# Branch products of a gated merge as fp16 products of Strassen's scheme, with all engines of the merge in written order

## The chip, the core and the metric

The kernel runs on one core of one Trainium2 chip. Its engines each have a queue of their own: TensorE (PE, matmuls; its weight loads are shown apart as PEld), VectorE (DVE), ScalarE (ACT), GpSimd (POOL), and SyncE (SP), which issues the DMAs. The metric is the device time of one execution in microseconds (us), as the median of the runs.

## The reference

One decoder layer for 512 positions and 16 meta tokens, width 1024, all in float32. Two attention branches (MLA and FoX, 16 heads of 64 each) are multiplied with gates and merged:

```python
y_mla = (o_mla * jax.nn.silu(z_mla)) @ w_br_mla[l]
...
y_fox = (o_fox * jax.nn.silu(z_fox)) @ w_br_fox[l]

mixed = (jax.nn.sigmoid(gate_a) * y_mla + jax.nn.sigmoid(gate_b) * y_fox) @ w_out[l]
h = h + rmsnorm(mixed, post_norm_g[l])
```

`gate_a` and `gate_b` are 1024 columns each of the projection `u @ w_in`. The change concerns the two products with `w_br_mla` and `w_br_fox`, each 512 x 1024 by 1024 x 1024, and the order of the work around them.

## The kernel before

Features lie on the partitions in tiles of 128, positions on the free axis. Float32 factors are cut into a high and a low part of type f32r (`wh`, `wl` for weights; `gh`, `gl` for activations), and a product is three matmuls per tile of 128 input features: high x high, high x low, low x high. A *unit* (`unit`) is one output tile of 128 features: 8 input tiles x 3 = 24 matmuls of 512 columns. Its weights come by a DMA of 512 KB into `wraw` (three buffers), ACT casts them to `wh` (L116), POOL subtracts to get `wl` (L92).

The stages in order: norm and small projections; attention, 16 stages of one head pair each (branch 1 is FoX, 0 is MLA), in which PE's order is written by hand and units of later work fill the time that the softmax takes; the merge; the output projection (`po`) with norm and store. In attention the weighted values are `ov` (fp16 matmuls, two heads in 64 columns each), and DVE writes `gT[br]` from them (L676), 128 x 8 x 512 f32 for each branch. The probabilities `pn` go through DMA transposes to `pt`, issued by SP.

There are 16 gate units (`pg`: tanh of half the gate goes to `th` on ACT, L409); four run in attention. The merge cuts `gT` into `gh`, `gl`, and then for each output tile i runs two branch units (`py`), multiplies on DVE (`tb`, L767), adds the branches (L770), cuts the sum into `mh` (ACT) and `ml` (DVE), and runs two of the gate units that are left. A scheduler sets the order of DVE, ACT, POOL and SP there; PE's order is that of the code.

Of the kernel before, what the change touches and what calls it, by code (L numbers as in the profile page):

```python
# [54 lines left out]
def block_kernel(ctx: ExitStack, tc: tile.TileContext, x, meta_tokens, pre_norm_g, w_in, fox_forget_b,  # L55
# [19 lines left out]
    uTh, uTl = (const.tile([128, KD, ROW + L - META], F32R, tag=n, name=n)[:, :, ROW - META :] for n in ("uTh", "uTl"))  # L75
    padp = ctx.enter_context(tc.tile_pool(name="padp", bufs=1, side="right"))
# [11 lines left out]
    def tps(*a):  # L88
        nc.tensor.transpose(*a)  # L89

# [60 lines left out]
    cqk = cctx.enter_context(tc.tile_pool(name="cqk", bufs=1, side="right"))  # L151
# [248 lines left out]
    gctx = ExitStack()  # L400
    gates = [(i, br) for i in range(KD) for br in range(2)]

    def gate_unit():

        i, br = gates.pop(0)

        def done(_, ps):
            ths[i, br] = thp.tile([128, S], F32, tag="th", name=f"th{i}{br}")
            nc.scalar.activation(ths[i, br], ps, AF.Tanh, scale=0.5)  # L409
        return unit(f"pg{i}{br}", win_w((O_GA, O_GB)[br], i), u_act, KD, REAL, done)  # L410


    with ExitStack() as att:
# [30 lines left out]
        gpool = gctx.enter_context(tc.tile_pool(name="gpool", bufs=1, side="right"))  # L444
        gT = [gpool.tile([128, KD, S], F32, tag=n, name=n) for n in ("gT0", "gT1")]
# [131 lines left out]
        def attention(br, pr):  # L577
# [88 lines left out]
            def values():  # L666
                po = ovp.tile([128, 512], F32, tag="ov", name=f"ov{nm_}")
                ph = [po[64 * h : 64 * h + 64] for h in range(2)]
                for h in range(2):
                    mm(ph[h], vms[br][0:80, h], pts[h][0:80, 0], start=True, stop=False)  # L670
                for j in range(4):
                    for i, (v, p) in enumerate(((0, 0), (0, 1), (1, 0))):
                        for h in range(2):
                            mm(ph[h][:, 128 * j :], vps[br][:, j, h, v], pts[h][:, 1 + 2 * j + p, 128 * j :], start=False,
                               stop=(j == 3 and i == 2))
                nc.vector.scalar_tensor_tensor(out=gT[br][:, pr, :], in0=po, scalar=vsc[br, pr], in1=sils[br, pr],  # L676
                                               op0=ALU.mult, op1=ALU.mult)

# [22 lines left out]
        for si, (br, pr) in enumerate(stages):  # L701
# [3 lines left out]
            if br == 1:  # L705

                za, zb = z_unit(1, pr), z_unit(0, pr)
                fill = za + vts[br, pr] + q + zb[:4] + k + zb[4:6] + v + zb[6:]
            elif not last:
                fill = q[:3] + vts[br, pr] + q[3:] + k + v  # L710
            else:
                g = gate_unit()
                fill = g[:4] + vts[br, pr] + g[4:] + gate_unit()
# [8 lines left out]
        ahead(first + sum(fills, []) + tail)  # L722
# [15 lines left out]
        run(tail[:4])  # L738
        va()
# [3 lines left out]
    fctx.close()  # L743
    rctx = ExitStack()
    with ExitStack() as mg:
        m1 = mg.enter_context(tc.tile_pool(name="m1", bufs=1))
        m2 = mg.enter_context(tc.tile_pool(name="m2", bufs=2))
        gh, gl = ([m1.tile([128, KD, S], F32R, tag=f"{n}{br}", name=f"{n}{br}") for br in (1, 0)][::-1]
                  for n in ("gh", "gl"))
        for br in (1, 0):  # L750
            for k in range(KD):
                nc.scalar.copy(gh[br][:, k], gT[br][:, k])
                split_lo(nc.vector, gl[br][:, k], gT[br][:, k], gh[br][:, k])
        gctx.close()
        cctx.close()
        mp = rctx.enter_context(tc.tile_pool(name="mp", bufs=1, side="right"))
        mh = mp.tile([128, KD, S], F32R, tag="mh", name="mh")
        ml = mp.tile([128, KD, S], F32R, tag="ml", name="ml")
        for i in range(KD):
            tb = {}  # L760
            for br in (1, 0):
# [3 lines left out]
                def done(_, py, br=br):  # L765
                    tb[br] = m2.tile([128, S], F32, tag=f"tb{br}", name=f"tb{i}{br}")
                    nc.vector.scalar_tensor_tensor(out=tb[br], in0=ths[i, br], scalar=1.0, in1=py, op0=ALU.add,  # L767
                                                   op1=ALU.mult)
                run(unit(f"py{i}{br}", get, lambda k, br=br: (gh[br][:, k, :], gl[br][:, k, :]), KD, [slice(0, S)], done))
            nc.vector.tensor_tensor(out=tb[0], in0=tb[0], in1=tb[1], op=ALU.add)  # L770
            nc.scalar.copy(mh[:, i], tb[0])
            split_lo(nc.vector, ml[:, i], tb[0], mh[:, i])
            for _ in range(2):
                if gates:
                    run(gate_unit())

        nc.scalar.activation(eps_t[0:1, 0:1], ths[KD - 1, 1][0:1, 0:1], AF.Square)
# [3 lines left out]
    with rctx, ExitStack() as og:  # L781
# [11 lines left out]

        def wout_unit(n, c, keep=None):
            return by_k(wunit([wout[:, 2 * c : 2 * c + 2, 512 * n : 512 * n + 512]], keep)[0], 2)
# [18 lines left out]
        for c in range(4):  # L814
            w = wout_unit(0, c)
# [68 lines left out]
```

## Time and profile before

| what | value |
|---|---|
| median of 3 runs | 632.11 us (631.9 to 633.5) |
| profiled execution, first to last instruction | 630.9 us |
| PE busy | 608.6 us (96%), granted clock 0.996 |
| PEld / DVE / ACT / POOL busy | 515.7 / 315.0 / 342.9 / 263.3 us |
| DMA queue | 84.67 MB, 53.0% of the engines' span |

The profiled execution's own time is known by its span alone; the runs lie 1.0 to 2.6 us above it, the median 1.2. The page gives busy time by engine, the chain that ended last (followed back from the last instruction through what released each step), groups of instructions with the mean length of one, and what ended the idle time before them. A matmul's length in the timeline includes its way through the array, so that neighbours overlap; the pace is read from start to start.

### The profile page before, as it was taken

Reading aid. Unit: us, or ns where it says so; the run is one execution under the profiler, and the core shown is the slowest. Engines: PE = TensorE matmul, PEld = TensorE weight load, DVE = VectorE, ACT = ScalarE, POOL = GpSimd, SP = SyncE. Lnnn points to the kernel's source line nnn. Section 1 sums busy time; section 2 is a strip of 40 time slices with the busy share of each in tenths; the row PEclk is TensorE's granted clock in tenths of the full one; section 3 lists DMA queues with packets and bytes.
Section 4 is the critical chain, followed back from the end, with each engine's and each line's share of the span. In section 5 each row is a group of like instructions: output and inputs, shape, how many; then the busy total and the mean of one; then the engine's idle time right before and its main releaser. Section 6 shows DMA issues by size and latency. Waiting matters only on the chain.

```text
span 630.9 us, 11084 instructions
## 1 busy us (share of the span) xinstructions
PE 608.6 (96%) x3890; PEld 515.7 (82%) x3890; DVE 315.0 (50%) x883; ACT 342.9 (54%) x774; POOL 263.3 (42%) x266
## 2 busy tenths in 40 slices
PE   3999989999999999999999999999999999999996
PEld 2879767988988889889889888878888888888885
DVE  3757557467476565674673765648222022113134
ACT  5656478378477575774784776757322232232321
POOL 3224633734344353343343443542544444444620
PEclk9999989999999999999999999999999999999999
DMA  8442657856656577467467665761532333333702
GB/s 284 123 84 54 138 147 188 205 143 153 168 135 137 145 148 163 113 162 174 101 157 175 116 153 149 158 166 38 162 93 80 97 99 100 101 100 113 255 34 100
DMA packets 204864, 85.38 MB, mean 135 GB/s; under 512 B 122684, under 2 KB 197820, under 8 KB 204808
## 3 DMA queue, kind: packets, MB, share of 16 engines
q1 hardware_dynamic: 204808, 84.67, 53.0%
q8 instruction: 30, 0.49, 0.3%
q14 instruction: 26, 0.21, 0.1%
HBM read 55.21 MB, written 4.26 MB: 94 GB/s over the span
## 4 chain that ended last, share of the span: by engine, by line
PE 89%; ACT 3%; DMA 3%; DVE 1%; issue 1%; POOL 1%; SPq 1%; DVEq 0%; POOLq 0%; ACTq 0%
PE py L86 14%; PE pg L86 14%; PE z L86 12%; PE v L86 8%; PE fk L86 7%; PE st L86 7%; PE po L86 7%; PE fq L86 7%; PE ov L86 5%; PE psm L86 3%; DMA pt<-pn 2%; PE mq L86 2%; PE mk L86 1%; PE vt L89 1%; DMA wsr<-in_w_in_dram 1%
## 5 line engine op out<-in xcount | busy, mean ns | idle before, releaser
L92 POOL TENSOR_TENSOR wl<-wraw,wh 128x1024 fp32r<-128x1024 f32 (+1 forms) x90 | 207.4, 2307 | 241.4 <-ACT wh L116 232.4
L116 ACT CAST wh<-wraw 128x1024 fp32r<-128x1024 f32 (+1 forms) x90 | 89.8, 1000 | 178.8 <-issue 84.1
L628 ACT ACTIVATE sf<-sf,nb 128x144 f32<-128x144 f32 (+3 forms) x128 | 71.9, 565 | 4.1 <-DVE nb L620 4.1
L655 ACT ACTIVATE pn<-sf,ri 128x128 f16<-128x128 f32 (+3 forms) x128 | 61.5, 551 | 15.0 <-ACT sf L628 14.8
L656 DVE SCALAR_TENSOR_TENSOR pn<-sf,ri,pn 128x128 f16<-128x128 f32 (+3 forms) x128 | 65.7, 553 | 7.9 <-ACT pn L655 7.9
L767 DVE SCALAR_TENSOR_TENSOR tb<-th,py 128x512 f32<-128x512 f32 x16 | 11.0, 686 | 107.4 <-PE py L86 107.4
L86 PE MATMUL z<-uTh,wh 128*128 128x512 f32 x128 | 51.4, 401 | 0.0
L86 PE MATMUL z<-uTh,wl 128*128 128x512 f32 x128 | 50.6, 395 | 0.0
L86 PE MATMUL z<-uTl,wh 128*128 128x512 f32 x128 | 50.4, 394 | 0.0
L86 PE MATMUL pg<-uTh,wh 128*128 128x512 f32 x128 | 50.1, 392 | 0.0
L86 PE MATMUL pg<-uTl,wh 128*128 128x512 f32 x128 | 49.8, 389 | 0.0
L86 PE MATMUL pg<-uTh,wl 128*128 128x512 f32 x128 | 49.8, 389 | 0.0
L86 PE MATMUL py<-gh,wh 128*128 128x512 f32 x128 | 49.8, 389 | 0.0
L86 PE MATMUL py<-gl,wh 128*128 128x512 f32 x128 | 49.8, 389 | 0.0
L86 PE MATMUL py<-gh,wl 128*128 128x512 f32 x128 | 49.8, 389 | 0.0
L620 DVE CUSTOM_DVE_ANT_0 sf<-st,maskt 128x272 f32<-128x272 f32 (+2 forms) x128 | 48.5, 435 | 0.0
L86 PE MATMUL st<-hlk,hlq 64*128 64x272 f32 (+3 forms) x480 | 48.0, 307 | 0.4 <-DVE nb L620 0.2
L642 POOL TENSOR_TENSOR mt<-sf,ri 128x96 f32<-128x96 f32 (+1 forms) x32 | 9.5, 297 | 83.7 <-DVE ri L637 62.1
L86 PEld LDWEIGHTS st<-hlk,hlq 64*128 64x128 f32 x480 | 35.4, 185 | 6.7 <-ACT wh L116 2.5
L86 PE MATMUL fk<-uTl,wh 128*128 128x256 f32 (+1 forms) x128 | 36.6, 286 | 0.0
L86 PE MATMUL fk<-uTh,wh 128*128 128x256 f32 (+1 forms) x128 | 36.5, 285 | 0.0
L86 PE MATMUL v<-uTh,wh 128*128 128x256 f32 (+1 forms) x128 | 36.5, 285 | 0.0
(186 smaller groups left out, 1449.4 us busy)
## 6 DMA issues: line engine op xcount, KB each, us to landing
wraw<-in_w_in_dram SPq DMA_DIRECT2D x56, 512.0 KB, 3.9
wraw<-in_w_br_fox_dram SPq DMA_DIRECT2D x8, 512.0 KB, 3.6
wraw<-in_w_br_mla_dram SPq DMA_DIRECT2D x8, 512.0 KB
wraw<-in_w_out_dram SPq DMA_DIRECT2D x8, 512.0 KB, 4.5
qpe_dram<-gT SPq DMA_DIRECT2D x8, 256.0 KB
QP<-qpe_dram SPq DMA_DIRECT2D x8, 256.0 KB, 2.8
pt<-pn SPq DMA_TRANSPOSE x128, 2.5
xr<-in_x_dram SPq DMA_DIRECT2D x4, 512.0 KB
```

What stands on the lines that cost most here:

```text
L86: nc.tensor.matmul(*a, **k)
L89: nc.tensor.transpose(*a)
L92: eng.tensor_tensor(out=lo, in0=src, in1=f32(hi), op=ALU.subtract)
L116: nc.scalar.copy(wh[:, :n], raw[:, :n])
L620: nc.vector.tensor_tensor_reduce(out=sf_of(h, b)[:, c0 : c0 + w], in0=ps[h][:, o : o + w], in1=maskt[:, m0 : m0 + w], scale=-scale, scalar ...
L628: nc.scalar.activation(sf, sf, AF.Exp, bias=sums["nb"][:, h, b : b + 1], scale=-1.0, accum_out=sums["su"][:, h, b : b + 1])
L642: nc.gpsimd.tensor_tensor(out=mt, in0=src, in1=ri.unsqueeze(3).broadcast_to([128, 2, nb_, META]), op=ALU.mult)
L655: nc.scalar.activation(hi, sf, AF.Copy, scale=rib)
L656: nc.vector.scalar_tensor_tensor(out=lo, in0=sf, scalar=rib, in1=hi, op0=ALU.mult, op1=ALU.subtract)
L767: nc.vector.scalar_tensor_tensor(out=tb[br], in0=ths[i, br], scalar=1.0, in1=py, op0=ALU.add, op1=ALU.mult)
```

## The change

The branch products `py` are made in another way. Two output tiles (a *pair*, 256 features) at a time, the 2 x 2 blocks of weights (halves of the input features by the two output tiles) and activations (halves of the features by halves of the positions) are combined by Strassen's scheme in Winograd's form: 7 products of blocks instead of 8. Each block or sum of blocks is scaled by a power of two and cut into two fp16 halves. A product is 4 input tiles x 3 matmuls of 256 columns. The scales come from the chip: ACT squares the data and sums along the rows (`sumsq`), a matmul with ones adds over the partitions (`total`, tiles `sum`), DVE keeps the exponent (`pow2_scale`, three or four small operations). Every sum of blocks is made in place, in `yraw` (raw weights, now 1 MB per DMA) by DVE, in `gT[1]` by POOL, in `gT[0]` by DVE. ACT makes the high half (`hi`), DVE the low half (`lo`). Results are added in three banks (`yx`, `yy`, `yz`; products 1, 6, 5, 3 add up in `yx`), with copies of partial results on ACT (`cp`, L940 to L944) and additions and gating on DVE (L821, L933). The two branches have different scales; `mixed` brings them together when `mh` and `ml` are cut.

In the merge the order of all five queues is now written out as a string of tokens: a digit is a product, `g` three matmuls of a gate unit, `G` the cast of a gate unit's weights, `ah1`/`al1` the high and low half of operand 1 for the next pair, `as` a sum, `aq` a square, `aS` a scale, `L` a load, `B1h1` the same for the activations of branch 1. The gate units are ordered by branch, FoX first; FoX's four pairs come first, then MLA's. One sum of blocks of `gT[1]` (POOL), its squares (ACT) and its scale are made in attention's last stages. The attention's own order is otherwise the same on each engine.

```diff
+    def sumsq(src, acc):
+
+        with nc.allow_low_precision(reason="a bound for a power of two"):
+            nc.scalar.activation(junk[:, : int(np.prod(src.shape[1:]))], src, AF.Square, accum_out=acc)
+
+    def total(cols):
+
+        ps = acc(f"sum{uid[0]}")[:, 0:1]
+        uid[0] += 1
+        for i, c in enumerate(cols):
+            mm(ps, ALL1, c, start=(i == 0), stop=(i == len(cols) - 1))
+        return ps
+
+    def pow2_scale(s, inv, sq):
+
+        nc.vector.tensor_scalar(out=inv.bitcast(I32), in0=sq.bitcast(I32), scalar1=0x7F000000, scalar2=1,
+                                op0=ALU.bitwise_and, op1=ALU.logical_shift_right)
+        nc.vector.tensor_scalar(out=inv, in0=inv, scalar1=2.0 ** 50, scalar2=2.0 ** -60, op0=ALU.mult, op1=ALU.max)
+        nc.vector.reciprocal(s, inv)
...
-    gates = [(i, br) for i in range(KD) for br in range(2)]
+    gates = [(i, br) for br in (1, 0) for i in range(KD)]
...
+                if br and pr % 2:
+                    g2 = gT[1][:, pr - 1 : pr + 1].rearrange("p k s -> p (k s)")
+                    sumsq(g2, gss[:, 1, pr // 2 : pr // 2 + 1])
...
+                def g_scale():
+                    pow2_scale(sg[1], isg[1], total([gss[:, 1, c : c + 1] for c in range(4)]))
+                    b1, b2 = (gT[1][:, 0:4, 256 * c : 256 * c + 256] for c in range(2))
+                    b22 = gT[1][:, 4:8, 256:512]
+                    nc.gpsimd.tensor_tensor(out=b2, in0=b22, in1=b2, op=ALU.subtract)
+                fill = g[:4] + vts[br, pr] + g[4:] + g2[:4] + [(100, g_scale)] + g2[4:]
...
-        for i in range(KD):
-            tb = {}
-            for br in (1, 0):
-                def get(br=br):
-                    return by_k(wunit([wbr[br][:, :, 128 * i : 128 * i + 128]])[0], KD)
...
-                run(unit(f"py{i}{br}", get, lambda k, br=br: (gh[br][:, k, :], gl[br][:, k, :]), KD, [slice(0, S)], done))
...
+        mg.enter_context(tc.manual_schedule(engines={E_.PE, E_.Activation, E_.DVE, E_.Pool, E_.SP}))
...
+            def hi(self, n):
+                t = self.pool.tile([128, 2, K2, self.width], F16, tag="op", name=f"{self.name}{n}")
+                nc.scalar.activation(t[:, 0], self.quads[n], AF.Copy, scale=self.s)
+                self.ops[n] = t
+
+            def lo(self, n):
+                t = self.ops[n]
+                nc.vector.scalar_tensor_tensor(out=t[:, 1], in0=self.quads[n], scalar=self.s, in1=t[:, 0], op0=ALU.mult,
+                                               op1=ALU.subtract)
...
+            def product(self, n):
+                ps = self.y if n in (7, 4) else self.z if n == 2 else self.x
+                a, b = W[self.br, self.p].ops[n], TB[self.br].ops[n]
+                first = n in (1, 7, 2)
+                q = 0
+                for k in range(K2):
+                    for i, j in ((0, 0), (0, 1), (1, 0)):
+                        mm(ps, a[:, i, k], b[:, j, k], start=(first and q == 0), stop=(q == 3 * K2 - 1),
+                           skip_group_check=not first)
+                        q += 1
...
+        std = ("1 {0} 7 2 aS 6 ah1 ah7 al1 g ah2 al7 g 4 as6 {2} al2 ah6 g as5 ah4 g 5 as3 al6 ah5 g bq0 al4 g ah3 3 bs7 "
+               "al5 g bq1 {1} al3 g cL")
...
+        go(2, std.format("J2", "J3 B0s7", "G"))
...
+        go(5, std.format("M00", "M01", "G"))
+        go(6, std.format("M10", "M11", ""))
+        go(7, "1 7 O 6 M20 2 O 5 M21 4 O 3 M30 M31")
```

How the order of three queues changes at the places that matter below. First PE, where a gate unit meets branch work; before, at the first branch unit:

```order
L86 MATMUL pg_5472<-uTh,wh_5468 128x512
L86 MATMUL pg_5472<-uTl,wh_5468 128x512
L86 MATMUL pg_5472<-uTh,wl_5469 128x512
L86 MATMUL py_5589<-gh_5540,wh_5585 128x512
L86 MATMUL py_5589<-gl_5542,wh_5585 128x512
L86 MATMUL py_5589<-gh_5540,wl_5586 128x512
```

PE now, in the first pair, at the end of product 6 (`aop` is an operand of weights, `bop` of activations, both fp16):

```order
L92 LDWEIGHTS aop_5678
L92 MATMUL yx_5705<-bop_5637,aop_5678 128x256
L92 MATMUL pg_5770<-uTh,wh_5627 128x512
L92 MATMUL pg_5770<-uTl,wh_5627 128x512
L92 MATMUL pg_5770<-uTh,wl_5628 128x512
```

f32r and fp16 now alternate within every pair; before, PE stayed with f32r. Next DVE, from the last `gT` to the first merged tile before:

```order
L676 SCALAR_TENSOR_TENSOR gT_678<-ov_5485,vsc_5223,sil_5244 128x512
L92 TENSOR_TENSOR gl_5542<-gT_679,gh_5540 128x512 x8
L92 TENSOR_TENSOR gl_5543<-gT_678,gh_5541 128x512 x8
L767 SCALAR_TENSOR_TENSOR tb_5614<-th_5422,py_5589 128x512
L767 SCALAR_TENSOR_TENSOR tb_5647<-th_791,py_5622 128x512
L770 TENSOR_TENSOR tb_5647<-tb_5647,tb_5614 128x512
L92 TENSOR_TENSOR ml<-tb_5647,mh 128x512
```

DVE now, at the end of the first pair (`cp_5708<-yx_5705` is the addition of product 5):

```order
L836 SCALAR_TENSOR_TENSOR bop_5768<-gT_687,gsc,bop_5768 128x1024
L836 SCALAR_TENSOR_TENSOR aop_5774<-yraw_5584,ysc_5586,aop_5774 128x512
L821 TENSOR_TENSOR yraw_5588<-yraw_5588 128x4x128
L821 TENSOR_TENSOR cp_5708<-yy_5706,cp_5708 128x256
L112 TENSOR_SCALAR ysc_5590<-sum_5816 128x1
L114 TENSOR_SCALAR ysc_5590<-ysc_5590 128x1
L115 RECIPROCAL ysc_5590<-ysc_5590 128x1
L880 TENSOR_SCALAR ysc_5590<-ysc_5590,gsc 128x1
L836 SCALAR_TENSOR_TENSOR aop_5823<-yraw_5588,ysc_5590,aop_5823 128x512
L821 TENSOR_TENSOR cp_5708<-yx_5705,cp_5708 128x256
L933 SCALAR_TENSOR_TENSOR th_5436<-th_5436,cp_5708 128x512
```

That addition, which frees the bank for product 3, stands behind the scale and the first low half of the second pair. Last ACT, before, from the end of attention on:

```order
L409 ACTIVATE th_5525<-pg_5472 128x512
L752 CAST gh_5540<-gT_679 128x512 x4
L752 CAST gh_5541<-gT_678 128x512 x8
L116 CAST wh_5654<-wraw_5652 128x1024
L116 CAST wh_5687<-wraw_5685 128x1024
L116 CAST wh_5720<-wraw_5718 128x1024
L771 CAST mh<-tb_5647 128x512
```

ACT now, for the operands of the second pair (`aop_5823` to `aop_5876`) up to the copies of that pair's first products:

```order
L831 ACTIVATE aop_5823<-yraw_5588,ysc_5590 128x512
L831 ACTIVATE aop_5825<-yraw_5588,ysc_5590 128x512
L831 ACTIVATE aop_5828<-yraw_5588,ysc_5590 128x512
L831 ACTIVATE aop_5846<-yraw_5588,ysc_5590 128x512
L831 ACTIVATE aop_5853<-yraw_5588,ysc_5590 128x512
L100 ACTIVATE junk,yss_5785<-yraw_5782 128x1024
L831 ACTIVATE aop_5858<-yraw_5588,ysc_5590 128x512
L831 ACTIVATE aop_5876<-yraw_5588,ysc_5590 128x512
L448 ACTIVATE th_5883<-pg_5770 128x512
L940 COPY cp_5893<-yx_5890 128x256
L942 COPY cp_5893<-yy_5891 128x256
```

The copy of product 1 of the second pair stands behind all seven high halves of that pair, a square and a tanh.

More of the change, by code (lines that the diff above doesn't have):

```diff
@@ L150, in block_kernel @@
     cctx = ExitStack()
[L151 removed]
+    cqk = cctx.enter_context(tc.tile_pool(name="cqk", bufs=1))
     cTh = cqk.tile([128, 3, L], F32R, tag="cTh", name="cTh")
@@ L720, in block_kernel @@
         tail = gate_unit()
-        ahead(first + sum(fills, []) + tail)
+        mgates = [Gate() for _ in gates[:]]
+        ahead(first + sum(fills, []) + tail + mgates[0].steps)
         run(first)
@@ L738, in block_kernel @@
         run(tail[:4])
+        mgates[0].make()
+        mgates[1].load()
         va()
@@ new lines, in block_kernel, with mixed @@
+        mix = {}
+        pre = []
+        def mixed(p, part):
+            w = W[0, p]
+            for i in (2 * p, 2 * p + 1):
+                m = ths[i, 1]
+                if part == 0:
+                    nc.vector.scalar_tensor_tensor(out=m, in0=m, scalar=w.r, in1=ths[i, 0], op0=ALU.mult, op1=ALU.add)
+                    nc.scalar.activation(mix["h"][:, i], m, AF.Copy, scale=w.inv)
+                else:
+                    nc.vector.scalar_tensor_tensor(out=mix["l"][:, i], in0=m, scalar=w.inv, in1=f32(mix["h"][:, i]),
+                                                   op0=ALU.mult, op1=ALU.subtract)
```

209 lines of the change are left out of this document (178 added, 31 removed).

## The prediction

> **What bounds the kernel now.** I read the chain that ended last first, then the busy time by stretch, then single instructions. The chain, in order of time (start, length, what; us):
>
> ```profile
> 424.32 1.97 PE ov L86 x26
> 426.29 2.95 PE pg L86 x12
> 429.24 10.88 PE py L86 x48
> ...
> 559.80 21.76 PE py L86 x96
> 581.56 43.92 PE po L86 x216
> ```
>
> Between the last attention matmul (`ov`) and the output projection (`po`) it is nothing but gate units (`pg`) and branch units (`py`). Busy time by engine in that stretch (PE, PEld, DVE, ACT, POOL, clock, DMA share, GB/s):
>
> ```profile
> 426.20:581.40 155.20, 155.20 (x688) 128.53 (x685) 41.84 (x46) 50.16 (x67) 69.74 (x28) 1.00 0.34 96
> ```
>
> PE is never idle there, DVE is busy for 27% and ACT for 32%, and the DMA engines for a third. So the merge lasts as long as its matmuls: `py` is six pieces of 10.88 and one of 21.76, 87.04 us for 384 matmuls of 512 columns (0.2267 us each), `pg` the other 68. A change of `py` counts in full for as long as the other engines keep up.
>
> **The products on PE.** 384 f32r matmuls of 512 columns become 8 pairs x 7 products x 12 = 672 fp16 matmuls of 256. Pace is start to start, since the lengths overlap. fp16 in `ov`, and f32r of 256 columns near the end, from the timeline (start, length, instruction):
>
> ```profile
> 425.63 0.49 PE L86 MATMUL ov<-pt,vp 128*64 128x256 f16 x6
> 425.74 0.44 PE L86 MATMUL ov<-pt,vp 128*64 128x256 f16 x6
> ...
> 425.96 0.33 PE L86 MATMUL ov<-pt,vp 128*64 128x128 f16 x5
> ...
> 622.84 0.28 PE L86 MATMUL po<-wh,mh 128*128 128x256 f32 x1
> ...
> 625.20 0.28 PE L86 MATMUL po<-wl,mh 128*128 128x256 f32 x1
> ```
>
> Three fp16 steps of 256 columns take 0.33 us, 0.110 each (two heads side by side in 64 columns). Twenty f32r steps take 2.36, 0.118 each. fp16 weights are half as wide, so I take 0.110: 672 x 0.110 = 73.9 us, **-13.1**; at 0.118 it would be 79.3, -7.7.
>
> Weight loads have their own row (the second figure is the mean in ns):
>
> ```profile
> L86 PEld LDWEIGHTS py<-gh,wh 128*128 128x128 f32 x128 | 24.0, 188 | 5.0
> L86 PEld LDWEIGHTS <-vp 128*64 128x64 f16 x384 | 21.2, 110 | 8.4
> ```
>
> For f32r a load of 188 ns stands in every 227 ns of a stream in which 512 columns alone take 217 (fp16, below): loads go on behind matmuls. The Trainium skill, "TensorE: Matmul & The Clock Gate", section "The mechanism" of Part 3, says that loads overlap matmuls in flight only when they go to another row group. Its section "Back-to-back issue gap" gives 81 ns for 128 columns and 131 for 512, from which 98 ns for 256 is an estimate of that page and 672 of them 66 us, a gain of 21. The trace agrees with neither: full-height loads hide, and the 512-column steps stand at 217 ns below. The rows decide.
>
> **Changes of number type.** After `ov` PE changes between f32r and fp16 56 times (28 each way). What a change costs, from rows:
>
> ```profile
> 412.72 0.60 PE L89 MATMUL vt<-ident,vT 128*128 128x128 f32 x4
> 413.15 0.27 PE L89 MATMUL vm<-ident,vT 128*128 128x128 f32 x1
> 413.50 0.40 PE L86 MATMUL pg<-uTl,wh 128*128 128x512 f32 x1
> ...
> 423.94 0.39 PE L86 MATMUL pg<-uTh,wl 128*128 128x512 f32 x1
> 424.25 0.41 PE L86 MATMUL ov<-pt,vm 80*64 80x512 f16 x2
> 424.49 0.39 PE L86 MATMUL ov<-pt,vp 128*64 128x512 f16 x2
> ...
> 426.22 0.50 PE L86 MATMUL pg<-uTh,wh 128*128 128x512 f32 x1
> 426.56 0.39 PE L86 MATMUL pg<-uTl,wh 128*128 128x512 f32 x1
> ```
>
> Plain f32 transposes come 0.108 apart (four in 0.43). From the last of them to the second `pg` matmul are 0.35 us, of which 0.108 and 0.227 are the two at their pace: 0.016 for the change. Into `ov` it is dearer: 0.31 and 0.24 instead of 0.227 and 0.217, 0.11 more; out of it 426.22 less 425.96 less three steps of 0.055, 0.10, and 0.34 instead of 0.227, 0.11: 0.31 for a round trip. But `ov` loads half the array's columns, the new products all of them, as the transposes do. So 0.03 each, nearest to the full-width row: **+1.7**; ends 56 x 0.016 = 0.9 and 28 x 0.31 = 8.7.
>
> **Sums for the scales.** 24 matmuls of one column with a weight load each. No row has such; nearest are the transposes at 0.108 (2.6) and 128 columns of fp16 at 0.055 (1.3). I take **+2.0**.
>
> **The cuts on ACT, DVE and POOL.** Their prices (line, engine, operation, tiles, count, then busy us and mean ns of one, idle before):
>
> ```profile
> L655 ACT ACTIVATE pn<-sf,ri 128x512 f16<-128x512 f32 x32 | 21.5, 715 | 7.3 <-ACT sf L628 7.1
> L322 ACT ACTIVATE hn<-ht 128x1024 f32<-128x1024 f32 x3 | 3.2, 1060 | 0.0
> L808 ACT ACTIVATION_READ_ACCUMULATOR jk<-po 128x1 f32 x9 | 1.7, 194 | 0.0
> L116 ACT CAST wh<-wraw 128x1024 fp32r<-128x1024 f32 x80 | 83.6, 1048 | 159.7 <-issue 82.6 <-PE py L86 33.9 <-PE pg L86 17.6
> L409 ACT ACTIVATE th<-pg 128x512 f32<-128x512 f32 x16 | 9.4, 589 | 0.0
> L228 ACT CAST hlk<-fk 128x256 fp32r<-128x256 f32 x8 | 2.9, 364 | 0.0
> L656 DVE SCALAR_TENSOR_TENSOR pn<-sf,ri,pn 128x512 f16<-128x512 f32 x32 | 22.7, 748 | 7.9 <-ACT pn L655 7.9
> L325 DVE SCALAR_TENSOR_TENSOR hn<-ht,st,gb 128x1024 f32<-128x1024 f32 x3 | 3.8, 1279 | 0.0
> L92 DVE TENSOR_TENSOR gl<-gT,gh 128x512 fp32r<-128x512 f32 x16 | 9.8, 685 | 0.9 <-ACT gh L752 0.8
> L92 DVE TENSOR_TENSOR ml<-tb,mh 128x512 fp32r<-128x512 f32 x8 | 16.9, 2112 | 5.5 <-ACT mh L771 5.5
> L810 DVE TENSOR_TENSOR yo<-po,gp 128x256 f32<-128x256 f32 x2 | 0.8, 425 | 2.7 <-ACT jk L808 2.7
> L534 DVE TENSOR_SCALAR vsc<-vsc 128x1 f32<-128x1 f32 x16 | 2.5, 154 | 0.6
> L92 POOL TENSOR_TENSOR wl<-wraw,wh 128x1024 fp32r<-128x1024 f32 x80 | 194.3, 2432 | 217.9 <-ACT wh L116 212.6 <-DMA pt<-pn 3.5 <-PE po L86 1.8
> ...
> 437.26 8.01 POOL L92 TENSOR_TENSOR wl<-wraw,wh 128x1024 fp32r<-128x1024 f32 x3 [12.29 <-ACT wh L116]
> 440.88 2.14 DVE L770 TENSOR_TENSOR tb<-tb,tb 128x512 f32<-128x512 f32 x1
> ```
>
> Note the two TENSOR_TENSOR rows of DVE: the same 512 elements take 0.69 us when POOL is idle and 2.1 while POOL has one of its own, as the last two rows show side by side.
>
> An ordinary pair then costs: PE 84 x 0.110 + a gate unit 5.44 + 0.4 = 15.1. ACT 7 high halves x 0.715, 2 squares x 1.25, 3 copies x 0.364, tanh 0.589, `wh` 1.048: 10.2. DVE 7 low halves x 0.748, 4 sums x 0.685, the scale 4 x 0.154, 5 operations on 256 columns x 0.425, one of 512 x 0.748: 11.5. Both fit behind PE, which is why I cost them at nothing there. Cover is thin at two places.
>
> *The start (pairs 0 and 1).* Count from the last `ov` matmul (t = 0). The halves of gT1 write into memory that attention still holds, so they begin behind its last DVE instruction:
>
> ```profile
> 426.40 0.75 DVE L676 SCALAR_TENSOR_TENSOR gT<-ov,vsc,sil 128x512 f32<-128x512 f32 x1 [8.02 <-PE ov L86]
> ```
>
> at 0.9. ACT has three halves of 1024, a tanh and two squares: 3.2 + 0.6 + 2.5, at 7.2. PE comes to the first sum at 2.7 + 21 x 0.227 = 7.5: no wait. It has 27 gate matmuls until 13.9, and the first cut is ready at about 11.8: no wait. In pair 0 product 3 waits for DVE's addition of product 5 (both use one bank), and in DVE's queue that stands behind the first low half of pair 1. From 11.1 on, DVE has 8 low halves (6.0), 3 of 1024 (3.8), 4 sums (2.7, and 1.4 more for one beside POOL's `gT` sums), 3 x 0.425, a scale (0.6): 15.8, and ACT's high half after the scale 0.7; so 27.6, with the addition 28.0. PE is there at 13.9 + 6 x 1.32 + 21 x 0.227 + 0.5 = 27.1: wait 0.9. In pair 1 product 6 waits for the copy of product 1, which on ACT stands behind 7 more halves, a square and a tanh: from 27.1, 5.0 + 1.25 + 0.6 + 0.4 = 34.3 and 1 for DVE's sums between; PE arrives at 28.0 + 1.32 + 0.7 + 3.96 = 34.0: wait 1.3. The next addition, behind a sum beside `wl`: 1.0. Semaphores and the rest of pairs 1 to 3: 0.8. Together **+4.0**. Ends 1 and 8 (three more sums at 2.1).
>
> *Pairs 5 and 6.* Merging adds 4 x 0.748 to DVE and 0.3 to the scale: 14.8 of 15.1, and 16.2 with one sum beside `wl`. **+1.5**; ends 0 and 4.
>
> **Joints.** The first `po` matmul now waits for the gating of the last product (0.18 from PE to DVE as in the row above, 0.43, semaphores): **+0.7**. Before, nothing stood there. The transposes ahead of the last `ov`:
>
> ```profile
> L661 SPq DMA_TRANSPOSE pt<-pn x128: 1178/1247/2295, 86.6 to 421.0; - x128
> DMA to landing us min/median/max: 2.3/2.5/4.5
> ```
>
> The last is issued at 421.0 and lands 2.5 later, 0.7 before PE needs it. On SP a 1 MB load now stands among them: one more issue, at most the 1.2 of a transpose, and its bytes ahead of theirs. PE itself comes 0.3 later, by its four sums. **+0.3**; ends 0 and 3 (the longest landing instead of the median, and an issue). Four squares of 1.25 in attention delay ACT's `pn`; in the first three of those stages five units stand between scores and `ov` where the last has three, and in the last SP's 1.2 per transpose is what sets the landing: nothing.
>
> Sum: -13.1 + 1.7 + 2.0 + 4.0 + 1.5 + 0.7 + 0.3 = **-2.9**. The profiled execution's span of 630.9 becomes 628.0; the median of the runs lies 1.2 above that span, so 632.1 becomes **629.2 us**.
>
> **Rivals.**
> - *The cuts hide wholly.* The DVE and ACT terms (5.5) fall away if DVE's sums seldom meet POOL, which in an ordinary pair has only 2.4 of 15.1 us. For it, a row of the same operation (least, median and greatest ns):
>
> ```profile
> L770 DVE TENSOR_TENSOR tb<-tb,tb x8: 691/692/2139, 440.9 to 582.3; 128x512 f32<-128x512 f32 x8
> ```
>
> Most of these met no POOL. Against: `ml` met it each time. 629.2 - 5.5 = 623.7 us. Chance 0.22.
> - *A change of type costs what it costs around `ov`* (ends on the other side): 8.7 instead of 1.7, so 636.2. It decides from (2.9 + 1.7) / 28 = 0.16 us a round trip. For it: the three rows of `ov`, the only fp16 there is. Against: the transposes. Chance 0.14.
> - *DVE becomes the bound:* two of four sums meet POOL in each pair, 11.5 + 2 x 1.4 = 14.3 and in merging pairs 17.6 against PE's 15.1. Pairs 5 and 6 then cost 5.0 instead of 1.5, and one more dear sum in the first pairs 1.4: 634.1. For it: `ml`. Against: POOL's 2.4 in 15.1. Chance 0.17.
> - *Loads do not hide behind fp16 matmuls of 256 columns.* At the 110 ns of the `vp` row each product matmul would take 0.22: 74 more, 703. The f32r streams speak against it. Chance 0.02. The rule of the Trainium skill on row groups, cited above, would have it so.
> - *No change:* the products run at 0.118, 5.4 dearer, and the start's waits of 4.0 lie behind that: -1.5. Chance 0.03.
>
> **The numbers.** My forecast has 0.42; its own range is 625 to 633. 0.3% is 1.9 us, about what a measurement tells from none. Faster: 0.22 and 0.27 of mine, 0.49. Same: 0.11 of mine, 0.05 of the third rival, 0.03: 0.19. Slower: 0.04, 0.14, 0.12, 0.02: 0.32. The range: 621.5 (cuts hidden, changes at 0.016, sums at 1.3) to 638 (`ov`'s price and a little more waiting).
>
> **What would show it.** The products' steps at 0.110 in the timeline, and PE's busy time in the merge near 145; idle PE before `po` of 0.7; idle PE of 1 to 2 us in each of the first two pairs, ended by DVE's `cp` addition and ACT's `cp` copy; `yraw` sums on DVE with a mean between 0.7 and 1.1. It is wrong if steps after a gate start 0.1 or more late, if `yraw` sums take 2 us throughout, or if PE waits in pairs 2 to 4.

## The result, and the profile after

The changed kernel took 651.7 us (median of four runs, 648.7 to 653.0) where the kernel before took 632.5. The medians lie 19.2 us apart; the ratio over the single executions, which the table below uses too, is 1.0286 (95% interval 1.0254 to 1.0319), or 18.1 us more. The forecast was 2.9 less, and the range ended at 638. The profiled execution took 650.5, with a span of 648.7.

The chain of work that ended last, after the change, at the places that were shown of before (start, length, what; us):

```profile
431.90 2.02 PE ov L92 x22
...
476.40 0.60 DVE yraw L821
477.00 2.79 DVE aop L836
479.80 0.60 DVE yraw L821
480.40 0.35 DVE cp L821
480.78 1.47 PE yx L92 x12
482.26 1.40 PE pg L92 x6
483.66 1.32 PE yx L92 x12
484.98 1.31 PE yy L92 x12
...
505.49 0.13 PE sum L92 x6
...
596.49 46.73 PE po L92 x216
```

Where the chain of before was nothing but matmuls, VectorE (DVE) now stands in it. Cut at the end of `ov` and the start of `po`, the span has three stretches: the last `ov` ends 7.6 us later (433.92 for 426.29; forecast 0.3), the merge is 7.3 longer (162.57 for 155.27; forecast 3.2 shorter), `po` 2.8 longer (46.73 for 43.92; forecast no change). These sum to 17.7 of the spans' 17.8.

Busy time in the merge (columns as in the prediction), then PE's waits there, in all, times, longest:

```profile
433.90:596.50 162.60, 146.76 (x994) 118.39 (x993) 143.59 (x210) 103.12 (x166) 45.78 (x17) 1.00 0.30 90
```
```profile
PE yx L92 <- DVE cp L821: 7.6, 6, 2.9
PE po L92 <- DVE th L933: 4.5, 1, 4.5
PE yx L92 <- ACT cp L940: 2.2, 3, 1.7
...
PE yy L92 <- DVE aop L836: 1.3, 1, 1.3
```

PE has 146.76 us of work, near the forecast (145), and stands idle for 15.8 more. For 13.6 of these it waits for DVE: six times for the addition that frees a product's bank, once for the gating ahead of `po`, and for operands; the other 2.2 are ACT's copies. What makes DVE late shows where two engines are read side by side, in the second pair, while the third pair's operands are cut (timeline):

```profile
475.33 0.74 DVE L836 SCALAR_TENSOR_TENSOR aop<-yraw,ysc,aop 128x512 f16<-128x512 f32 x1
...
476.87 2.38 POOL L118 TENSOR_TENSOR wl<-wraw,wh 128x1024 fp32r<-128x1024 f32 x1 [12.94 <-ACT wh L142]
476.92 2.87 DVE L836 SCALAR_TENSOR_TENSOR aop<-yraw,ysc,aop 128x512 f16<-128x512 f32 x1
...
480.32 0.41 DVE L821 TENSOR_TENSOR cp<-yx,cp 128x256 f32<-128x256 f32 x1
...
480.78 1.47 PE L92 MATMUL yx<-bop,aop 128*128 128x256 f16 x12 [0.98 <-DVE cp L821]
```

A low half of this size takes 0.74 us alone and 2.87 beside one of POOL's weight subtractions. POOL's ends at 479.25, the low half at 479.79, 0.54 later, as if it had stood still until POOL was done. Behind it in DVE's queue is the addition into `cp`, and behind that PE. Over all such low halves (line, engine, operation, count: least, median, greatest ns):

```profile
L836 DVE SCALAR_TENSOR_TENSOR aop<-yraw,ysc,aop x56: 737/744/2881, 445.8 to 584.0; 128x512 f16<-128x512 f32 x56
```

They are busy for 55.5 us, 13.8 more than 56 at the median. The Trainium skill has this ("SBUF — State Buffer", section "Who interferes with whom"): a DVE instruction with two inputs in SBUF and a GpSimd one that reads SBUF exclude each other, and the first holds the way for its whole length. The rows agree; an addition into `cp`, one of whose inputs lies in PSUM, keeps its 0.42 beside POOL in the next rows (at 589.47).

At the end of the merge (timeline):

```profile
589.40 5.11 POOL L118 TENSOR_TENSOR wl<-wraw,wh 128x1024 fp32r<-128x1024 f32 x2 [0.17 <-PE yx L92]
589.47 0.42 DVE L821 TENSOR_TENSOR cp<-yx,cp 128x256 f32<-128x256 f32 x1
589.81 5.24 DVE L969 SCALAR_TENSOR_TENSOR ml<-th,ysc,mh 128x512 fp32r<-128x512 f32 x2
594.97 0.41 DVE L821 TENSOR_TENSOR cp<-yy,cp 128x256 f32<-128x256 f32 x1
...
596.49 0.76 PE L92 MATMUL po<-wh,mh 128*128 128x512 f32 x1 [4.51 <-DVE th L933]
597.05 0.63 PE L92 MATMUL po<-wh,ml 128*128 128x512 f32 x1
```

Two `ml` are held for 5.24 us by the split of the output projection's weights, and the last addition and the gating of the last two products stand behind them. After the wait of 4.5 us the first eight `po` matmuls come about 0.43 apart, then 0.23 (the granted clock is 0.51 from 596.5 to 600.0); this is called a slow start below, and it costs 1.6 us of `po`'s 2.8.

### The profile page after: what moved, and what is told of

It is laid out like the page before. It is cut to its first block, busy times and chain, and to the rows that moved or that the text cites. A ratio compares the mean times of both kernels' runs of the same rounds, so it can differ in the third digit from the quotient of the medians.

```text
span 648.7 us, 11930 instructions
## 1 busy us (share of the span) xinstructions
PE 607.7 (94%) x4202; PEld 508.7 (78%) x4202; DVE 417.8 (64%) x1050; ACT 400.7 (62%) x884; POOL 238.8 (37%) x256
## 5 line engine op out<-in xcount | busy, mean ns | idle before, releaser
L118 POOL TENSOR_TENSOR wl<-wraw,wh 128x1024 fp32r<-128x1024 f32 (+1 forms) x74 | 168.5, 2280 | 269.4 <-ACT wh L142 261.4
L142 ACT CAST wh<-wraw 128x1024 fp32r<-128x1024 f32 (+1 forms) x74 | 72.8, 986 | 79.5 <-issue 39.1
L92 PEld LDWEIGHTS <-aop 128*128 128x128 f16 x672 | 63.2, 98 | 27.6 <-issue 18.3
L836 DVE SCALAR_TENSOR_TENSOR aop<-yraw,ysc,aop 128x512 f16<-128x512 f32 x56 | 55.5, 1018 | 3.4 <-ACT aop L831 3.4
L92 PE MATMUL yx<-bop,aop 128*128 128x256 f16 x384 | 47.6, 273 | 10.1 <-DVE cp L821 7.6
L92 PE MATMUL pg<-uTh,wh 128*128 128x512 f32 x128 | 53.4, 417 | 0.0
L831 ACT ACTIVATE aop<-yraw,ysc 128x512 f16<-128x512 f32 x56 | 37.6, 715 | 25.3 <-DVE yraw L821 22.7
L572 DVE TENSOR_REDUCE vsc<-v 128x1 f32<-128x272 f32 (+1 forms) x32 | 13.1, 431 | 37.0 <-PE v L92 37.0
L92 PE MATMUL v<-uTh,wl 128*128 128x256 f32 (+1 forms) x128 | 36.5, 286 | 0.0
L92 PE MATMUL v<-uTl,wh 128*128 128x256 f32 (+1 forms) x128 | 36.5, 285 | 0.0
```

The costliest lines, as they stand in the source:

```text
L92: nc.tensor.matmul(*a, **k)
L118: eng.tensor_tensor(out=lo, in0=src, in1=f32(hi), op=ALU.subtract)
L142: nc.scalar.copy(wh[:, :n], raw[:, :n])
L572: nc.vector.tensor_reduce(out=sc[:, i : i + 1], in_=ps, op=ALU.max, axis=AX.X, apply_absolute_value=True)
L831: nc.scalar.activation(t[:, 0], self.quads[n], AF.Copy, scale=self.s)
L836: nc.vector.scalar_tensor_tensor(out=t[:, 1], in0=self.quads[n], scalar=self.s, in1=t[:, 0], op0=ALU.mult, op1=ALU.subtract)
```

## The experiments

All runs, with the time as a ratio to the kernel before on the same chip (its medians lie between 632.3 and 633.5 us), and the three stretches of the profiled execution (end of the last `ov`; from there to the first `po`; `po`):

| kernel | median us | ratio, 95% interval | `ov` ends | merge | `po` |
|---|---|---|---|---|---|
| before | 632.5 | 1 | 426.29 | 155.27 | 43.92 |
| after | 651.7 | 1.0286 (1.0254 to 1.0319) | 433.92 | 162.57 | 46.73 |
| x3_dve | 645.9 | 1.0185 (1.0151 to 1.0219) | 432.58 | 157.84 | 47.53 |
| x4_end | 646.2 | 1.0199 (1.0177 to 1.0220) | 433.39 | 160.99 | 45.24 |
| x7_copy | 634.9 | 1.0045 (1.0027 to 1.0063) | 433.28 | 149.06 | 45.24 |
| x1_pad | 646.8 | 1.0225 (1.0191 to 1.0259) | 428.48 | 162.55 | 47.64 |
| x2_shift | 639.5 | 1.0090 (1.0062 to 1.0118) | 430.57 | 157.42 | 44.96 |
| x5_pad256 | 648.9 | 1.0256 (1.0230 to 1.0282) | 432.20 | 162.98 | 47.08 |
| x9_both | 647.8 | 1.0225 (1.0192 to 1.0259) | 427.61 | 164.75 | 46.59 |
| x11_pn128 | 634.2 | 1.0019 (1.0000 to 1.0038) | 430.89 | 155.27 | 43.92 |
| x6_g1sum | 651.0 | 1.0296 (1.0262 to 1.0330) | 434.48 | 164.19 | 46.80 |
| x12_s7 | 649.4 | 1.0260 (1.0227 to 1.0294) | 432.54 | 162.59 | 46.80 |
| x14_load | 655.7 | 1.0350 (1.0319 to 1.0380) | 432.02 | 168.56 | 48.04 |
| x8_all | 628.5 | 0.9946 (0.9926 to 0.9966) | 431.41 | 146.09 | 43.96 |
| x10_all2 | 625.4 | 0.9892 (0.9852 to 0.9932) | 426.87 | 146.08 | 43.95 |
| x13_load | 629.5 | 0.9927 (0.9903 to 0.9952) | 428.22 | 149.21 | 43.95 |
| x15_noaddr | 631.2 | 0.9969 (0.9947 to 0.9991) | 430.20 | 146.37 | 44.99 |
| x16_again | 628.2 | 0.9914 (0.9887 to 0.9941) | 431.09 | 146.08 | 43.96 |

**POOL beside DVE.** `x3_dve` gives the gates' weight subtractions in pairs 1 to 5 to DVE, most of them at the end of a pair.

```
-        split_lo(nc.gpsimd, wl[:, :n], raw[:, :n], wh[:, :n])
+        if hold[0]:
+            held.append(lambda: split_lo(nc.vector, wl[:, :n], raw[:, :n], wh[:, :n]))
+        else:
+            split_lo(nc.gpsimd, wl[:, :n], raw[:, :n], wh[:, :n])
...
-        go(2, std.format("J2", "J3 B0s7", "G"))
+        go(2, std.format("J2", "J3 B0s7", "G") + " D")
```

> The changed kernel, with eight of the gate units' subtractions wl taken from POOL to VectorE, most of them to the end of a pair, where VectorE stands idle for 2 us. Theory L (a VectorE instruction with two SBUF inputs stands still until POOL's two-input instruction has ended): the low halves and sums of 2.8 us go back to 0.75 and 0.69, 15 us of VectorE less against 8 x 1.25 = 10 us more; PE's waits for cp in pairs 1 to 4 (1.0, 2.9 and 0.7 us) go, with their cold restarts: 645 to 648 us. Theory F (VectorE is simply full, its own work is the bound): 10 us more work on it, so PE waits longer: 653 to 661 us.

The merge fell by 4.7 us, and the time came as expected. PE's waits say where the rest stayed:

```profile
PE po L93 <- DVE th L937: 4.6, 1, 4.6
PE pg L93 <- DVE wl L119: 3.3, 3, 1.3
...
PE yx L93 <- DVE cp L825: 1.2, 1, 1.2
```

The waits for `cp` are nearly gone (7.6 to 1.2), the end is as it was, and the subtractions are themselves late in DVE's queue. There an addition passes POOL unhindered, while the `ml` behind it do not:

```profile
580.72 7.62 POOL L119 TENSOR_TENSOR wl<-wraw,wh 128x1024 fp32r<-128x1024 f32 x3 [94.94 <-ACT wh L143]
...
583.29 0.41 DVE L825 TENSOR_TENSOR cp<-yx,cp 128x256 f32<-128x256 f32 x1
583.63 5.25 DVE L973 SCALAR_TENSOR_TENSOR ml<-th,ysc,mh 128x512 fp32r<-128x512 f32 x2
```

`x4_end` writes the first split of the output projection's weights at the end of pair 6 and the two others behind the last product, and moves two `ml` (M21) behind the last product's gating. `P` is now the load of such weights, `O` their split.

```
-        go(6, std.format("M10", "M11", ""))
-        go(7, "1 7 O 6 M20 2 O 5 M21 4 O 3 M30 M31")
+        go(6, std.format("M10", "M11", "P") + " O")
+        go(7, "1 7 P P 6 M20 2 5 4 3 M21 O O M30 M31")
```

> The changed kernel, with only the last pair in another order: the low halves ml of M21 behind product 3's gating, the first output unit made at the end of pair 6 and the two others behind M21. Theory: the 4.5 us before the first po is product 3's gating queued behind two ml that POOL's wl held up (5.2 us for the two); it falls to 0.7 to 1.2 us, and the eight po matmuls at 0.427 us after it go at full pace (1.6 us): 645.5 to 647.5 us. Rival: po then waits for its own weights or for ACT's casts instead, and the time stays at 650 to 652 us.

The wait before `po` fell from 4.5 to 1.3 us; the last two splits still stretch one gating to 1.62 us, but the two `ml` that they hold (3.21) now stand behind the last gating. `po` has no slow start any more, and its 45.24 are 1.3 above before, of which the addresses below make 1.0. Merge and `po` together fell by only 3.1, because this execution has a slow start elsewhere: from 498.3 to 501.1, after a wait of 2.86 us, the granted clock is 0.50, which costs 1.5. In the profile of `after` the same wait of 2.85 is followed by a clock of 1.00. So whether a wait of this length has a slow start behind it differs from one execution to another, and stretches of the table can differ by 1.5 us and more for that alone.

`x7_copy` puts a copy in place of each of POOL's weight subtractions from the merge on, so it leaves out the low halves of those weights.

```
-        split_lo(nc.gpsimd, wl[:, :n], raw[:, :n], wh[:, :n])
+        if hold[0]:
+            nc.gpsimd.tensor_copy(wl[:, :n], raw[:, :n])
+        else:
+            split_lo(nc.gpsimd, wl[:, :n], raw[:, :n], wh[:, :n])
```

> The changed kernel, with POOL's subtraction wl = wraw - wh of the gate and output weights in the merge replaced by a copy of wraw into wl (one input, same tile, same place in POOL's queue). It leaves the low halves of these weights out of the computation; the sums of quarters stay as they were. Theory L2 (VectorE stands still beside a two-input instruction of POOL only): the six aop of 2.8 us in pairs 1 to 6 go back to 0.75, the wait for cp of 2.9 and 0.7 us goes, the two ml before po take 1.4 instead of 5.2 us: 642.5 to 645.5 us. Theory P (any POOL instruction on a large tile holds VectorE up): they stay at 2 us or more, 650 to 652 us.

This one edit takes back 0.0241 of the ratio, 15.2 us (0.0251 against `x6_g1sum`, a repeat of `after` on the same chip), and in the profile 15.0 of merge and `po`; it came 7.6 us below the least that was expected of it. But it does not show that only a POOL instruction with two inputs holds DVE, since copies held it too, for their own shorter length, and where one began while DVE was at work it was POOL that waited (a copy alone takes 1.04):

```profile
467.00 1.34 POOL L145 CAST wl<-wraw 128x1024 fp32r<-128x1024 f32 x1 [17.22 <-DMA wraw<-in_w_in_dram]
467.36 1.52 DVE L840 SCALAR_TENSOR_TENSOR aop<-yraw,ysc,aop 128x512 f16<-128x512 f32 x1
...
490.50 2.12 POOL L145 CAST wl<-wraw 128x1024 fp32r<-128x1024 f32 x1 [3.92 <-DMA wraw<-in_w_in_dram]
```

The copies are also released by the load and not by ACT's high half, so they start earlier, and none met the last four `ml`; two of the earlier four took 1.5.

**Addresses.** The change adds constants of 2400 bytes of a partition, among them a tile `gss` of 32, and the tiles behind them go from multiples of 64 bytes to odd multiples of 32. `x1_pad` makes the constants 2432 bytes, `x5_pad256` 2560, ten times 256; `x9_both` is `x5_pad256` with 128 bytes ahead of the attention pool, which puts `pn` and `pt` at multiples of 256 again. `x2_shift` and `x11_pn128` move tiles in the kernel before and change nothing else. The comments name the runs:

```
-    gss = const.tile([128, 2, 8], BF16, tag="gss", name="gss")
+    gss = const.tile([128, 2, 16], BF16, tag="gss", name="gss")      # x1_pad; 48 in x5_pad256 and x9_both
...
+    const.tile([128, 8], F32, tag="shift", name="shift")             # x2_shift, in before
...
+        ac.tile([128, 32], F32, tag="shift", name="shift")           # x9_both; x11_pn128, in before
```

> The changed kernel, with the 32-byte tile gss made 64 bytes wide and nothing else. The new constants (gss 32, gsc 64, ALL1 256, junk 2048 bytes of a partition) moved every tile behind them from a multiple of 64 bytes to an odd multiple of 32. Theory A (addresses): the 512-column fp32r matmuls go back from 0.2337 to 0.2267 us, that is 2.0 us in the 300 gate matmuls behind the last ov and 1.0 us in the 168 of po, and the 1.3 us by which the attention drifts between its second stage and its last; if the transposes that are 3 us late near 100 us come from the addresses too, 3.8 us more. So 643.5 to 647.5 us. Theory B (this one execution was slow by chance): 651.7 us within 0.3%, paces of 0.2337 as before.

> The kernel before, with an unused tile of 32 bytes ahead of its padding, so that its tiles stand at odd multiples of 32 bytes, and nothing else. Theory A: 384 gate, 384 branch and 168 output matmuls at 0.2337 instead of 0.2267 us are 6.5 us, and 1.3 us in the attention: 640 us, with the late transposes 644 us. Theory B: 632 us within 0.3%.

> The changed kernel, with gss widened until the new constants take 2560 bytes of a partition, ten times 256, instead of 2400. With 2432 bytes (a multiple of 64) the transposes came in time again but the gate matmuls still took 0.2324 us; in the kernel before shifted by 32 bytes the gate matmuls, whose activations uTh did not move with their weights, took 0.2334, and the branch matmuls, of which both operands had moved by 32, 0.2271. Theory D (the pace of an fp32r matmul hangs on the distance of its two operands' addresses within 256 bytes): gate and output matmuls at 0.2267 us, 3.1 us less than with 2432 bytes (646.8), so 643 to 644.5 us. Rival (the pace belongs to the chip or to the program's mix): 0.2324 as with 2432 bytes, 646 to 647.5 us.

> The changed kernel with constants of 2560 bytes and an unused tile of 128 bytes ahead of the attention's own tiles, so that pn and pt stand at multiples of 256 bytes again, as before the change. With constants of 2560 bytes alone the gate matmuls took 0.2267 us, but pn stood 128 bytes off, the queues moved 215 GB/s beside the transposes instead of 290, and the first ov came 2.9 us late. Theory T (a transpose whose rows of 256 bytes straddle two lines of 256 is a third slower): the first ov's gating within 0.5 us of before, DMA share 0.64 to 0.65 over 60 to 430 us instead of 0.69, and 3.5 us less than 648.9: 644 to 646 us. Rival (the late transposes come from the chip or the run): 648 to 650 us, share 0.69.

> The kernel before with an unused tile of 128 bytes ahead of the attention's tiles: pn, pt and what follows them in the attention move by 128 bytes, weights, activations and branch operands stay. Theory T: DMA share 0.69 instead of 0.64, first ov about 3 us late, the pace of gate, branch and output matmuls 0.2267 us as before: 635 to 636.5 us. Rival: 632.3 us within 0.3%.

`x2_shift`: 32 unused bytes make the kernel before 5.7 us slower, of which merge and `po` hold 3.2. There the f32r matmuls of one program have two lengths (ns):

```profile
L87 PE MATMUL py<-gh,wh x4: 389/389/389, 485.8 to 487.8; 128*128 128x512 f32 x4
...
L87 PE MATMUL pg<-uTh,wh x5: 395/396/396, 496.2 to 499.0; 128*128 128x512 f32 x5
```

Start to start these are 0.227 and 0.233. The operands of `py` both moved by 32 bytes, of those of `pg` only one. Over all runs the pace in long rows of f32r matmuls goes with the distance of the two operands' addresses modulo 256: 0.2265 to 0.2278 at zero, 0.2324 to 0.2342 at 32, 96 and 128. Between fp16 products the distance shows nothing; `x16_again` (distance zero), chain:

```profile
531.41 6.85 PE pg L93 x30
...
549.01 1.40 PE pg L93 x6
```

Thirty gate matmuls there take 0.228 each, but six between two products 1.40, as in `after` (482.26 above), where the distance is 96. The transposes react to another thing, the place of the attention's tiles, `pn` and `pt` among them (stretch 60 to 430 us; the last two columns are DMA share and GB/s; before, after, `x11_pn128`):

```profile
60.00:430.00 370.00, 365.57 (x2740) 312.06 (x2740) 226.27 (x734) 244.48 (x592) 159.45 (x204) 1.00 0.64 151
```
```profile
60.00:430.00 370.00, 364.44 (x2707) 309.63 (x2706) 226.14 (x733) 246.20 (x596) 160.71 (x205) 0.99 0.70 149
```
```profile
60.00:430.00 370.00, 363.73 (x2710) 310.39 (x2710) 222.79 (x728) 242.07 (x586) 158.84 (x204) 0.99 0.69 149
```

With `pn` at a multiple of 256 bytes the same traffic keeps the DMA engines busy for 0.63 to 0.65 (six kernels), elsewhere for 0.69 to 0.71 (twelve). What that is worth in time is less clear: `x11_pn128` has the dear transposes alone, and its median is 1.05 us above before, with an interval from none to 0.38%. In the changed kernel `x5_pad256` gains 0.004 of the ratio against `x6_g1sum` on the same chip, which lies within the two intervals, and `x9_both` 0.006 against `after`. `x5_pad256` has the pace that was expected of it but missed its time by 4.4 us: PE idles 15.9 us of its merge, as in `after`, and its profile has two slow starts worth 4.4 us where that of `after` has one of 1.7. `x9_both` has its first `ov` and its DMA share as expected and is 1.8 us above its range. `x1_pad` came in its range for another reason than the one given first: its gates stay at 0.232, only its transposes came in time.

**The last transposes.** `x6_g1sum` was to move POOL's first sum of `gT1` away from the last `pn`. Its line moved, but in POOL's queue the sum kept its place, so it is a repeat of `after`, and agrees with it. `x12_s7` writes that sum into the merge's order, where it runs on POOL behind two weight subtractions and no longer beside the `pn`. `x14_load` holds the first load of `yraw` (1 MB) until the last `ov` is gated; `x13_load` does so in `x10_all2`.

```
-                    nc.gpsimd.tensor_tensor(out=b2, in0=b22, in1=b2, op=ALU.subtract)   # x6_g1sum, x12_s7
...
-        go(-1, "aL bL G B1h1 B1h7 ...
+        go(-1, "aL bL G B1h1 B1s7 B1h7 ...                                              # x12_s7
...
+                    nc.vector.tensor_copy(raw[:, 0, 0:1], gT[0][:, KD - 1, 0:1])        # x13_load, x14_load
```

> The changed kernel, with POOL's sum of two quarters of gT1 (128x1024, 2.4 us) taken out of the last attention stage and put behind the last output gate's weights, where VectorE is idle. Theory: the low half of pn that stood 2.2 us instead of 0.47 beside that sum goes back, the last transposes and the last ov come 1.75 us earlier: the last ov's gating stands 0.4 us later than the drift instead of 2.2, 649.5 to 650.3 us. Rival (the lag is ACT's square sum or the full DMA queues): 651.7 us within 0.3%.

> The changed kernel with the first sum of gT1's quarters in the merge's written order, behind the weights that POOL splits ahead of it (the run before this one, with the sum's line moved, had it at the same place in POOL's queue, since the attention's order is the scheduler's). Theory: the low half of pn in the last stage takes 0.47 instead of 2.22 us, the last ov comes 1.75 us earlier: 649 to 650 us. Rival (ACT's square sum or the queues hold the transposes up): 651 us, the last ov's gating 2 us behind the stage before as now.

> The changed kernel with the same held load and nothing else. Theory Q: the gap, 18.5 us here, falls to about 17 (the sum on POOL beside pn stays): 1.5 us less; but the first scale needs the load, about 438 us, which then lands at 436 to 438: 650 to 652 us. Rival: gap 18.5 us.

> The combined version (625.4 us) with the first load of the merge (yraw, 1 MB) held until the last ov's gating: one value of gT is copied into the tile ahead of the load, which overwrites it. Theory Q (the last transposes queue behind that megabyte): the gap from the last stage's gating to that of the stage before, which grew from 16.3 to 17.8 us, goes back to 16.3: 1.5 us less, if the load is not late for the first scale then; 623.9 us. Rival (the square sum on ACT holds the last pn up): 17.8 us stay, 625.4 us or, with the load late, up to 628.

From the gating of the stage before to the last gating are 16.29 us in `before`, 18.52 in `after`, 18.42 in `x12_s7`, and 16.87 in `x14_load`; in `x10_all2` (below) 17.8, and 16.55 with the load held (`x13_load`). So the load in SP's queue is worth 1.3 to 1.7: in `after` the six transposes behind it take 9.38 us to issue, in `x14_load` all eight 10.73, and in `before` 10.66. The sum beside `pn` is worth nothing that shows, though it held a `pn` for 2.22 us instead of 0.47: the seven kernels that keep it and have `pn` off the multiples of 256 lie between 18.25 and 18.52. The time of `x12_s7` came in its range without the cause that was given for it. Nothing is won by holding the load, since it and the gate weights behind it are then late (PE idles 4.1 us of the merge of `x13_load`), and both kernels end above what was expected. The chain of `x13_load`:

```profile
426.23 1.99 PE ov L93 x26
430.36 8.07 DMA wraw<-in_w_in_dram
```

**All of it together.** `x8_all` has POOL's merge subtractions and sums on DVE (all but the last two splits for `po` and the first sum), the weights of `po` split as in `x4_end`, the constants of `x5_pad256`, and the first banks of `po` taken from the gates' sums. `x10_all2` adds the 128 bytes of `x9_both` and moves the first sum as in `x12_s7`; `x16_again` is `x10_all2` once more, beside `x15_noaddr`, which lacks both paddings.

```
-                self.eng = (nc.vector, nc.gpsimd)[br]
+                self.eng = nc.vector
...
-              "al2 ah4 as3 al6 bq0 ah5 g 3 ah3 al4 al5 g al3 cL")
+              "al2 ah4 as3 al6 bq0 ah5 g 3 ah3 al4 al5 g al3 D cL")
```

> All of it together: constants of 2560 bytes, the sum of gT1 late, all subtractions and sums of the merge on VectorE, the last pair reordered, and the first three po accumulated in the banks of the gate sums so that they need not wait for the last gating. From 651.7: 8 us by the addresses, 5 to 6 by VectorE, 5.5 by the end, 1.75 by the sum, 1.3 to 2 by the banks: 628 to 631.5 us, the first version below the kernel before. Rival (VectorE, with 6 us more work in the first pair, holds PE up there): 632 to 637 us.

> The combined version (628.5 us) with the 128 bytes ahead of the attention's tiles and with the first sum of gT1's quarters in the merge's written order behind the last output gate's weights. Theory T and the sum's lock: 3.2 us by the transposes and 1.75 us by the sum: 622.5 to 625 us. Rival for each: 628.5 us if neither holds, 626.5 if only the sum does.

> The combined version without its two address paddings (gss 32 bytes wide, no 128 bytes in the attention), on the same chip as the combined version itself. Theory (addresses cost the change 4 us, as the runs of padded and unpadded kernels on different chips say): 629 to 630 us against 625.4. From the paces alone (300 gate matmuls by 0.007, 168 output matmuls by 0.006, 1.3 us of drift): 4.4 us. If the late first transposes of the profiled executions are in every execution: 8 us, 633 us. Rival (the paddings do nothing outside the profile): 625.4 us within 0.3%.

> The combined version again, word for word, on the same chip as the three others of this call, so that they can be compared with it: 624 to 627 us.

The best version takes 0.9892 and, on another chip, 0.9914 of the time of before: it beats both kernels. `x8_all` came in its range, `x10_all2` 0.4 us above it, the two others 1.2. Merge and low halves, in `x16_again` and `x8_all`:

```profile
431.00:577.00 146.00, 144.48 (x995) 118.22 (x993) 128.27 (x221) 103.66 (x166) 2.37 (x2) 1.00 0.31 97
```
```profile
L842 DVE SCALAR_TENSOR_TENSOR aop<-yraw,ysc,aop x56: 744/746/754, 441.8 to 569.5; 128x512 f16<-128x512 f32 x56
```

PE idles 1.5 us of the merge's 146.0, where it idled 15.8. DVE does more work than in the changed kernel (eleven subtractions of 1.22 and the sums), and is busy for 15.3 us less. `x15_noaddr` is 3.0 us slower than `x16_again` on the same chip; 1.3 of that stands in merge and `po`.

## Why the prediction was wrong, by its steps

The step that failed is the price of the cuts: "DVE 7 low halves x 0.748 ... Both fit behind PE, which is why I cost them at nothing there." The prediction saw that POOL's instructions stretch DVE's, from 0.69 us to 2.1, but took that for TENSOR_TENSOR alone and so for the sums alone. Low halves, `ml` and gating, SCALAR_TENSOR_TENSOR with both inputs in SBUF, were priced as if alone. There are 56 `aop` low halves to 32 sums of `yraw`. The sums came out as forecast, 0.75 on average; the `aop` low halves at 1.02, those of `bop` at 1.62 for 1.28. So PE waited 6.3 us in pairs 2 to 4 (2.9, 0.7 and 2.8), where the text said that this would show it wrong; in `x16_again`, with POOL out of the way, 0.9. The rival "DVE becomes the bound" named the mechanism, with the sums only, and stopped at 634.1.

- *Products:* right. Twelve matmuls take 1.31 to 1.33, 0.110 each.
- *Changes of type:* at most 0.6 or about 1.3 for 1.7, by the pace that is taken. Six `pg` at this kernel's pace of 0.234 are 1.40, which is what stands between two products, and a product behind a gate takes 1.33 for 1.31: 28 x 0.02 is 0.6. But the prediction counted gates at 0.227, and six of these are 1.36. A product (1.31) and six gates take 2.72 us here and in `x16_again` alike, so against 0.227 a round trip costs 0.05, and 28 of them 1.3. The runs do not separate the price of a change from the pace of short rows.
- *Sums for the scales:* six in 0.13, so 24 in 0.5 for 2.0.
- *Start (4.0):* in pairs 0 and 1 PE idles 4.3, near the forecast in part by luck. The two `cp` additions cost 2.2 for 1.9, the second behind a low half beside POOL and not behind a sum; ACT's copies 0.6 for 1.3; and 1.5 is a wait for operands, for which no term stood. In `x16_again` the two pairs idle 0.6.
- *Pairs 5 and 6 (1.5):* 0.7, and none in `x16_again`.
- *First `po`:* 0.7 forecast, 4.5 measured, and 2.8 more in `po`, 1.6 of it the slow start and 1.0 the addresses. What was missed is the split of `po`'s weights beside `ml`, though the prediction's own row showed `ml` at 2.1 beside POOL.
- *Transposes ahead of the last `ov`:* 0.3 forecast, 2.2 measured between the last two gatings, inside the ends given; at most 1.7 of it is the load.
- *Missing:* the addresses, 3 to 4 us by `x9_both` and `x15_noaddr`. No term stood for them.

In merge and `po`, 10.1 us over before became 9.1 under it in `x16_again`, with POOL out of the way, the end in another order and the addresses put right: 5.9 better than the 3.2 forecast. What stays open is the rest of the 7.6 us by which the last `ov` ended late. The first `ov` was already 3.8 late, and that differs from execution to execution of the same kernel (0.8 early in `x10_all2`, 2.7 late in `x16_again`), so a single profile cannot settle it. Over all eighteen profiles its gating ends at 101.6 to 105.1 us in the six kernels with `pn` at a multiple of 256 bytes and at 103.3 to 106.2 in the others, so the place of `pn` probably has a part in it; how large it is the runs do not show.

## What to carry to other kernels

Before an engine's work is priced as hidden, list for each of its instructions where its operands lie and what runs beside it: on DVE, each one with two inputs in SBUF has to be priced twice, alone and beside POOL. Work given to an idle POOL is not free if a busy DVE is the cover; here the kernel got faster when DVE did POOL's share as well. And a small tile among the constants moves everything behind it, so compare the addresses of matmul operands and of transposed tiles before and after.

## What the hardware showed that was not expected

- The lock takes in SCALAR_TENSOR_TENSOR (0.74 to 2.87 us) and POOL's one-input copies (DVE 0.75 to 1.52, or the copy itself 1.04 to 2.12).
- f32r matmuls of 512 columns, in long rows, run at 0.227 or 0.233 us by the distance of their operands' addresses modulo 256 bytes, 3% for 32 unused bytes; in rows of six between fp16 products no difference shows.
- After a wait of 2.9 us the granted clock was 0.50 for 2.8 us in `x4_end` and 1.00 in `after`.
- Transposes between tiles that do not start at a multiple of 256 bytes keep the DMA engines busy for 0.70 instead of 0.64 of the time, for the same bytes.
